# q of the odd heads by Strassen products ahead of the recurrence, and weight sums of the gates issued late

## The chip, the cores and the metric

The kernel runs on one core of a Trainium2 chip. The metric is the device time of one execution in microseconds; of several executions the median counts. The core has engines that work side by side, each through its own instructions in a fixed order: TensorE (PE: matmuls; its weight loads are shown apart as PEld), VectorE (DVE), ScalarE (ACT), GpSimd (POOL) and SyncE (SP). POOL and SP here mostly issue DMAs. An engine waits for another by semaphores.

## The reference

Two layers over 512 tokens with 16 meta tokens ahead of them (528 columns in the kernel), 2048 channels. The even layer joins a convolution module and a sparse attention of 8 heads, each multiplied by a gate, and projects the result out. The odd layer is a gated linear recurrence of 16 heads with a state of 128 by 128 each:

```python
def even_mixer(hn, w_in, ...):
    ...
    a_out = jax.nn.silu(layer_norm(u, ln_g, ln_b)) * jax.nn.silu(gate_a)
    ...
    b_out = b_out * jax.nn.silu(gate_b)
    return jnp.concatenate([a_out, b_out], axis=-1) @ w_out

def odd_mixer(hn, w_in, lb, norm_g, w_out):
    q, fz, i, g = split_last(hn @ w_in, (D_REC, D_REC, D_REC, D_REC))
    ...
    o = hgrn2_chunkwise(heads(jax.nn.silu(q)), heads(log_f), heads(k), heads(i))
    o = o * lax.rsqrt(jnp.mean(jnp.square(o), -1, keepdims=True) + RMS_EPS)
    ...
    return (o * silu(g)) @ w_out
```

All is float32. The change concerns q, one of the four projections of the odd layer: `hn @ w_in`, 2048 by 2048 for 512 tokens, 128 rows for each head.

## The kernel before

**Products in three matmuls.** To keep float32 precision each operand is split into a high half that TensorE takes as it is and a low half, the rest. `products` (L182 to L191) issues for each of eight slices of 128 channels three matmuls: high weights by high data (L188), high by low (L189), low by high (L190), 24 in all for one half stripe of weights (128 x 1024). `load_half` (L150 to L161) loads such a half on SP (L154), makes its high part on ACT (`wh`, L159) and its low part on DVE (`wl`, L160). `stripe` (L163) takes two halves for 128 rows of a projection.

**Strassen.** A pair of stripes against the two halves of the tokens (264 or 256 columns) can be had by seven products with half the columns, of sums of weights with sums of data ("forms": B11, B21, B22, N1, N2, T3, T4), where the plain way needs eight. The weight sums of products 7, 5, 6 and 3 are made in DRAM by `sum_step` (L246): a copying DMA (L258) and accumulating DMAs (L260) on POOL's queue. `some_steps` (L288) issues the next few of a list behind a given instruction. Lists: `steps` for the even layer's output, `gsteps` for q of the even heads and the output gates of heads 0 to 7 (`QPAIRS`, `GPAIRS`), `osteps` for the odd layer's output.

**Course of the program.** (1) The even layer's projections, scores, selection and the attention's heads; `gsteps` are issued behind steps of the scores, of the attention and of its last head (L551, L671, L735). (2) The eight gates of the convolution module (L774 to L787): `gate` (L604) runs a stripe, evacuates it with the norm's factor on DVE (L196), takes a tanh on ACT (L611) and multiplies on DVE (L612); then `z`, the module's output, is finished (L781 to L785). (3) The even layer's output projection: the pools of the attention are closed and a pool `xf` takes their place. `early_form0` makes the forms of the attention (tiles `sq`, loaded from DRAM by `attended` on POOL, L808, three buffers) and of `z`: high half `fh` on ACT (L205), low half `fl` on DVE (L206). The forms N2, N1, T3, T4 follow (L825 to L828, `xh` and `xl`). POOL also loads the residual (L844). Then 56 products in the order m = 2, 3, 1, 6, 5, 7, 4, each m for eight pairs (L864); what comes out is added to the residual on DVE, and `finish1` splits the new layer's input. (4) Head 0's projections, then Strassen products for q of the eight even heads and for eight gates (`strassen`, L982), from forms `gforms`; q of heads 12 and 14 goes to DRAM (`qd`), since there is no place for it. (5) The recurrence: for each of 16 heads `projections` (L950) runs the stripes fz, q (odd heads only) and v, and `rec_head` the recurrence itself; `head_inputs` (L1028) gives the tiles and loads q of heads 12 and 14 on SP. (6) Gates 8 to 15, forms, the odd layer's output by Strassen, the final norm.

**What sets the order.** A scheduler places instructions on each engine by a simulated timeline, with priority bands: weights (WGT) ahead of evacuation (EVAC), that ahead of SIDE (forms, pacing, heads' inner work) and CONV. Within an engine the order that comes out is fixed. Pools hold rings of buffers: a tile takes the place of an older one and waits for that one's last reader.

Of the kernel before, what the change touches and what calls it, by code (L numbers as in the profile page):

```python
# [72 lines left out]
def trunk_kernel(ctx: ExitStack, tc: tile.TileContext, x: bass.AP, w: bass.AP, wukv: bass.AP,  # L73
# [5 lines left out]
    def band(level):  # L79
        return tc.high_priority(level * 1000000)  # L80
# [171 lines left out]
    def sum_step(what, m, pair):  # L252

        a = {11: w[pair[0], 0], 12: w[pair[0], 1], 21: w[pair[1], 0], 22: w[pair[1], 1]}
        if what == "copy":
            dst = wsum[pair, m] = dram.tile([128, 1024], F32, name=f"ws{pair[0]}_{m}")
            src = {7: a[11], 5: a[21], 6: wsum.get((pair, 5)), 3: wsum.get((pair, 6))}[m]
            return (Q if m in (5, 7) and pair in EPAIRS else G).dma_start(dst, src)  # L258
        src = {7: a[21], 5: a[22], 6: a[11], 3: a[12]}[m]
        return G.dma_start(wsum[pair, m], src, accum_op=OP.add, max_dma_last_dim=4096)  # L260

    def product_weights(pair, m):
# [8 lines left out]
             for what, m in (("add", 7), ("add", 5), ("copy", 6), ("add", 6), ("copy", 3), ("add", 3))  # L271
             for pr in EPAIRS[g:g + 4]]
    QHEADS = tuple(range(0, 16, 2))
    QPAIRS = [tuple(S_FQV + 3 * h + 1 for h in QHEADS[i:i + 2]) for i in range(0, 8, 2)]
    GPAIRS = [(S_G + 2 * i, S_G + 2 * i + 1) for i in range(4)]
    gsteps = [(what, m, pr)
              for what, m in (("copy", 7), ("copy", 5), ("add", 7), ("add", 5),
                              ("copy", 6), ("add", 6), ("copy", 3), ("add", 3))
              for pr in QPAIRS]
    gsteps += [(what, m, pr)  # L280
               for what, m in (("copy", 7), ("copy", 5), ("add", 7), ("add", 5),
                               ("copy", 6), ("add", 6), ("copy", 3), ("add", 3))
               for pr in GPAIRS]
    osteps = [(what, m, pr) for pr in OPAIRS
              for what, m in (("copy", 7), ("copy", 5), ("add", 7), ("add", 5),
                              ("copy", 6), ("add", 6), ("copy", 3), ("add", 3))]
# [1 line left out]
    def some_steps(todo, n, behind):  # L288
        with tc.issue_after(behind.ins):
            for _ in range(min(n, len(todo))):  # L290
                sum_step(*todo.pop(0))

    def strassen_weights(pair, m, pool, at):

# [5 lines left out]
    bdram = dram.tile([HB, 16, BL], F32, name="bdram")  # L300
    mbd = dram.tile([HB, 128, T], F32, name="mbd")
    h1d = dram.tile([KT, 128, T], F32, name="h1d")
    qd = dram.tile([2, 128, SEQ], F32, name="qd")


    r1p = ctx.enter_context(tc.tile_pool(name="r1", bufs=KT, side="left", reuse_waits="tile"))
# [297 lines left out]
    def gate(s, dst, X, rstd, wide=True):  # L604

        ps = stripe(s, X, wide=wide)
        n = T if wide else SEQ
        a = et([128, T], F32, "gt", 3)
        with band(EVAC):
            evac(a[:, :n], ps, rstd)  # L610
            S.activation(dst, a[:, :n], AF.Tanh, scale=0.5)  # L611
            V.scalar_tensor_tensor(dst, dst, 1.0, a[:, :n], op0=OP.add, op1=OP.mult)  # L612
# [104 lines left out]
    def head(h):  # L717
        if h == 0:
            meta_tiles()
        if h % 2 == 0:  # L720
            with band(SIDE):
                kv.append(keys_values(h // 2))
        gb = et([128, T], F32, "gb", 2)
        gate(S_GQ + 2 * h, gb, X0, rstd0)
        ps = stripe(S_GQ + 2 * h + 1, X0)
        qh = et([128, T], F32, "qh", 2)
        with band(EVAC):
            evac(qh, ps, rstd0)
        Kh, Vt = [t[h % 2] for t in kv[-1]]
        with band(SIDE):  # L730
            for name, src in (("q", qh), ("k", Kh), ("g", gb)):
                S.activation(meta_of(name, h), src[:, :NM], AF.Copy)
            moved = G.dma_start(meta["v"][h * NM:(h + 1) * NM, :], Vt[:NM, 0, :])
            if h == HB - 1:
                some_steps(gsteps, 7, moved)  # L735
            if h == HB - 1:
                attend_meta()
            attend(h, qh, gb, Kh, Vt)
# [36 lines left out]
    for i in range(8):  # L775
        ga = et([128, T], F32, "gb", 2)
        gate(S_GA + i, ga, X0, rstd0)
        with band(SIDE):
            z = Z[i]
            V.tensor_tensor(z, z, rz, op=OP.mult)  # L780
            S.activation(z, z, AF.Identity, scale=col(V_LG + i), bias=col(V_LB + i))  # L781
            th = et([128, T], F32, "gt", 3)
            S.activation(th, z, AF.Tanh, scale=0.5)
            V.scalar_tensor_tensor(z, th, 1.0, z, op0=OP.add, op1=OP.mult)
            V.tensor_tensor(z, z, ga, op=OP.mult)  # L785
        MA.append(z)
# [79 lines left out]
    for at, (pr, m) in enumerate(turns):  # L866
        u, c0, c1 = us[pr], C[pr], C[8 + pr]
        o = (mps if at % 7 < 3 else ps1)()[:, :HT]
        with band(WGT):
            hi, lo = strassen_weights(EPAIRS[pr], m, xfp, at)  # L870
        products(o, hi, lo, forms0[FORM[m]], True, True)
        with band(EVAC):
            if m == 2:
                V.tensor_tensor(c0[:, LT], c0[:, LT], o, op=OP.add)
            elif m == 3:
                V.tensor_tensor(c0[:, RT], c0[:, RT], o, op=OP.add)
            elif m == 1:
                S.activation(u, o, AF.Copy)
                V.tensor_tensor(c0[:, LT], c0[:, LT], o, op=OP.add)
            elif m == 6:  # L880
                V.tensor_tensor(u, u, o, op=OP.add)
                V.tensor_tensor(c0[:, RT], c0[:, RT], u, op=OP.add)
            elif m == 5:
                V.tensor_tensor(c0[:, RT], c0[:, RT], o, op=OP.add)
                V.tensor_tensor(c1[:, RT], c1[:, RT], o, op=OP.subtract)
                finish1(pr)
            elif m == 7:
                V.tensor_tensor(u, u, o, op=OP.add)
                both = c1.rearrange("p (c t) -> p c t", c=2)
# [74 lines left out]
    def q_made(h):  # L964

        with band(EVAC):
            scaled(QT[h])
            if h >= 12:
                Q.dma_start(qd[h // 2 - 6], QT[h])

    def silu_gate(h):

# [6 lines left out]

    made = [0]  # L980

    def strassen(pairs, results, finished):  # L982

        act = None
        for m, pr in ((m, pr) for ms in ((1, 2, 3), (5,), (6,), (7,), (4,)) for pr in range(len(pairs)) for m in ms):
            o = (mps if made[0] % 7 < 3 else ps1)()[:, :HS]
            with band(WGT):
                hi, lo = strassen_weights(pairs[pr], m, gpp, made[0])
            made[0] += 1
            products(o, hi, lo, gforms[FORM[m]], True, True)  # L990
            (a, b), (aj, bj) = [[t[:, c * HS:(c + 1) * HS] for c in range(2)] for t in results[2 * pr:2 * pr + 2]]
            u = aj
            with band(EVAC):
                if m == 1:
                    S.activation(u, o, AF.Copy)
                elif m == 2:
                    V.tensor_tensor(a, u, o, op=OP.add)
                elif m == 3:
                    S.activation(b, o, AF.Copy)
                elif m == 5:  # L1000
                    V.tensor_tensor(b, b, o, op=OP.add)
                    S.activation(bj, o, AF.Copy, scale=-1.0)
                elif m == 6:
                    V.tensor_tensor(u, u, o, op=OP.add)
                    V.tensor_tensor(b, b, u, op=OP.add)
                    finished(2 * pr)
                elif m == 7:
                    V.tensor_tensor(u, u, o, op=OP.add)
                    V.tensor_tensor(bj, bj, u, op=OP.subtract)
                else:  # L1010
                    V.scalar_tensor_tensor(aj, u, -1.0, o, op0=OP.mult, op1=OP.subtract)
                    act = finished(2 * pr + 1)
        return act

    strassen(QPAIRS, [QT[h] for h in QHEADS], lambda n: q_made(QHEADS[n]))
    ON = [on_tile(h) for h in range(8)]
    act = strassen(GPAIRS, ON, silu_gate)
    with band(SIDE), tc.issue_after(act.ins):
        S.preload_act_table_set("natural_log_exp_and_others")
    gp.__exit__(None, None, None)  # L1020
# [6 lines left out]

    def head_inputs(h):  # L1028
        fz, v = [ht([128, T], F32, name, 2) for name in ("fz", "v")]
        if h in QT and h < 12:  # L1030
            return fz, QT[h], v
        q = ht([128, SEQ], F32, "q", 2)
        if h in QT:
            with band(WGT), tc.issue_after(loaded[0].ins):
                Q.dma_start(q, qd[h // 2 - 6])
        return fz, q, v

    hs = tc.tile_pool(name="hs", bufs=1, side="left", reuse_waits="tile")
# [505 lines left out]
```

## Time and profile before

| | |
|---|---|
| runs | 1882.87, 1882.13, 1880.12 us; median 1882.13 us |
| profiled execution | 1882.83 us, its span 1881.0 us |
| granted TensorE clock, mean | 0.998 |
| TensorE matmuls | 15347, busy 1864.0 us |
| DRAM traffic | 322.28 MB read, 112.41 MB written, 231 GB/s over the span |

A line of the page or of a view of the trace names an instruction by its line, engine, operation and the tiles that it writes and reads (`fl<-sq,fh`: fl from sq and fh), with its shape. A timeline row begins with the start and the duration in us; in brackets stands how long the engine sat idle before it and what it waited for. A row of the windows view begins with a stretch of the span and gives its length, the busy time of each engine with the number of its instructions, the granted clock, the mean share of the 16 DMA engines and GB/s. "L" numbers are lines of the kernel before; in the changed kernel the same code stands some lines further down (L205 and L206 stay, L612 is L622, L808 is L822, L844 is L858).

### The profile page before, as it was taken

The page shows a single profiled execution, that of the slowest core. Times are in us where ns is not written, and L with a number is a line of the kernel's source. Part 1 is how long each engine was busy: PE and PEld are TensorE (multiplying, and loading weights), DVE is VectorE, ACT ScalarE, POOL GpSimd, SP SyncE. Part 2 cuts the span into 40 slices and gives each one's busy share as a digit, 9 for nine tenths or more (in the row PEclk, how much of TensorE's full clock was granted, in tenths as well). Part 3 has the DMA queues.
Part 4 walks back from the last instruction along what each step waited for, and adds up shares of the span by engine and source line. Part 5 has one row for each costly group of instructions (what it writes and reads, how often), then busy time and mean ns, then how long its engine had stood idle before and what let it go on. Part 6 is the DMA issues. An engine that isn't in the chain of part 4 may idle for free.

```text
span 1881.0 us, 37954 instructions
## 1 busy us (share of the span) xinstructions
PE 1864.0 (99%) x15347; PEld 1792.7 (95%) x15347; DVE 1470.2 (78%) x2832; ACT 920.7 (49%) x1637; POOL 228.0 (12%) x379
## 2 busy tenths in 40 slices
PE   9999999999999999999999999999999999999997
PEld 8998899999999999999999999999999999889997
DVE  7599889997648569588875898878878787588777
ACT  6333532234433645456544655555555555346553
POOL 1020132123430212000000111000000100000000
PEclk9999999999999999999999999999999999999999
DMA  6578788889993857567655655534544544235665
GB/s 233 157 243 256 202 238 199 225 223 230 254 242 116 199 165 251 186 225 243 213 198 183 184 162 151 134 113 137 145 124 130 152 127 121 79 112 163 210 222 180
DMA packets 97776, 344.45 MB, mean 183 GB/s; under 512 B 14208, under 2 KB 22056, under 8 KB 96064
## 3 DMA queue, kind: packets, MB, share of 16 engines
q1 hardware_dynamic: 68272, 222.20, 35.2%
q0 software_dynamic: 29040, 119.63, 26.8%
q8 instruction: 120, 1.97, 0.4%
q14 instruction: 56, 0.46, 0.1%
q10 hardware_dynamic: 288, 0.19, 0.0%
HBM read 322.28 MB, written 112.41 MB: 231 GB/s over the span
## 4 chain that ended last, share of the span: by engine, by line
PE 92%; DVE 4%; DMA 2%; ACT 1%; issue 0%; SPq 0%; DVEq 0%; ACTq 0%
PE mps L189 22%; PE mps L188 22%; PE mps L190 22%; PE s L189 2%; PE s L188 2%; PE s L190 2%; PE sv L189 1%; DMA w<-in_w_dram 1%; PE sv L188 1%; PE sv L190 1%; PE po L703 1%; PE st L189 1%; PE st L188 1%; PE st L190 1%; PE s L1086 1%; DMA L<-mask 1%
## 5 line engine op out<-in xcount | busy, mean ns | idle before, releaser
L189 PE MATMUL mps<-xl,wh 128*128 128x264 f32 (+2 forms) x2928 | 883.2, 302 | 0.0
L188 PE MATMUL mps<-xh,wh 128*128 128x264 f32 (+2 forms) x2928 | 878.5, 300 | 2.5 <-DVE gt L196 2.1
L190 PE MATMUL mps<-xh,wl 128*128 128x264 f32 (+2 forms) x2928 | 880.8, 301 | 0.0
L159 ACT ACTIVATE wh<-w 128x1024 fp32r<-128x1024 f32 x361 | 382.7, 1060 | 545.1 <-PE mps L189 340.9
L188 PEld LDWEIGHTS mps<-xh,wh 128*128 128x128 f32 x2928 | 551.0, 188 | 20.5 <-DVE gt L196 2.7
L189 PEld LDWEIGHTS mps<-xl,wh 128*128 128x128 f32 x2928 | 551.6, 188 | 17.4 <-issue 0.6
L190 PEld LDWEIGHTS mps<-xh,wl 128*128 128x128 f32 x2928 | 551.1, 188 | 17.3
L160 DVE TENSOR_TENSOR wl<-w,wh 128x1024 fp32r<-128x1024 f32 x361 | 441.6, 1223 | 156.6 <-ACT wh L159 153.3
L600 DVE SCALAR_TENSOR_TENSOR z<-u,vec,z 128x528 f32<-128x528 f32 x240 | 181.1, 765 | 2.5
L260 POOL DMA_DIRECT2D ws<-in_w_dram x96 | 87.2, 1154 | 103.8 <-DMA ws<-ws 70.2
L189 PE MATMUL s<-xl,wh 128*128 128x256 f32 (+1 forms) x248 | 70.3, 283 | 0.0
L188 PE MATMUL s<-xh,wh 128*128 128x256 f32 (+1 forms) x248 | 70.2, 283 | 0.0
L190 PE MATMUL s<-xh,wl 128*128 128x256 f32 (+1 forms) x248 | 69.7, 281 | 0.0
L1169 DVE COPY_PREDICATED A<-msk,s 128x256 f32<-128x256 uint8 x96 | 47.0, 490 | 17.7 <-PE s L1088 16.9
L196 DVE TENSOR_TENSOR gt<-mps,rstd 128x264 f32<-128x264 f32 (+1 forms) x72 | 32.9, 458 | 30.4 <-PE mps L190 30.0
L663 POOL DMA_DIRECT2D L<-mask x32 | 30.3, 947 | 166.7 <-DMA L<-bdram 85.1
L1082 ACT ACTIVATE kt1h<-k 128x256 f16<-128x256 f32 x64 | 26.5, 414 | 42.7 <-DVE k L1175 41.9
L190 PEld LDWEIGHTS s<-xh,wl 128*128 128x128 f32 x248 | 46.8, 189 | 0.0
L189 PEld LDWEIGHTS s<-xl,wh 128*128 128x128 f32 x248 | 46.7, 188 | 0.1
L188 PEld LDWEIGHTS s<-xh,wh 128*128 128x128 f32 x248 | 46.7, 188 | 0.0
L1082 ACT ACTIVATE kt0h<-k 128x512 f16<-128x512 f32 (+1 forms) x64 | 33.0, 516 | 22.4 <-DVE k L1175 21.5
L565 DVE SCALAR_TENSOR_TENSOR mask<-sq,wiT,mask 128x264 f32<-128x264 f32 (+3 forms) x80 | 37.7, 494 | 7.1 <-ACT sq L564 6.2
(720 smaller groups left out, 3727.6 us busy)
## 6 DMA issues: line engine op xcount, KB each, us to landing
w<-in_w_dram SPq DMA_DIRECT2D x267, 512.0 KB, 3.9
ws<-in_w_dram POOLq DMA_DIRECT2D x128, 512.0 KB, 8.6
w<-ws SPq DMA_DIRECT2D x96, 512.0 KB, 3.5
ws<-ws POOLq DMA_DIRECT2D x48, 512.0 KB, 5.4
ws<-in_w_dram SPq DMA_DIRECT2D x16, 512.0 KB, 7.1
on<-h1d SPq DMA_DIRECT2D x30, 256.0 KB, 4.2
sq<-mbd POOLq DMA_DIRECT2D x16, 264.0 KB, 3.6
z<-in_x_dram SPq DMA_DIRECT2D x8, 264.0 KB, 4.9
```

Of the source, the lines that this page charges most:

```text
L159: S.activation(uh, used, AF.Copy)
L160: V.tensor_tensor(ul, used, uh.bitcast(F32), op=OP.subtract)
L188: P.matmul(o, hi[:, ws], xh, start=start and k == 0, stop=False)
L189: P.matmul(o, hi[:, ws], xl, start=False, stop=False)
L190: issued.append(P.matmul(o, lo[:, ws], xh, start=False, stop=stop and k == len(X) - 1))
L196: V.tensor_tensor(dst[:, sl.start - o:sl.stop - o], p[:dst.shape[0]], rstd[:dst.shape[0], sl], op=OP.mult)
L260: return G.dma_start(wsum[pair, m], src, accum_op=OP.add, max_dma_last_dim=4096)
L565: V.scalar_tensor_tensor(M[t][:, s0:s1], r[:, :s1 - s0], wiT[:, t, h:h + 1], M[t][:, s0:s1], op0=OP.mult, op1=OP.add)
L600: V.scalar_tensor_tensor(z, u[:, j:j + T], col(V_CW + i * CW + j), z, op0=OP.mult, op1=OP.add)
L663: return G.dma_start(biased[h, t][:, :wk(t)], M[t], accum_op=OP.add)
L1082: S.activation(hi, src, AF.Copy, scale=scale)
L1169: V.copy_predicated(A.rearrange("p b (n a m) -> p b n a m", a=2, m=mm)[:, :, :, 1, :], msk[:, li - 1 + i:li + i, :].rearrange("p b (n m) - ...
```

## The change

q of the odd heads, 8 stripes of 512 columns inside the recurrence, is now computed as four more pairs of Strassen products (`CPAIRS`) between those of the even heads' q and those of the gates. All eight results go to DRAM (`qd` has ten places), and `head_inputs` loads them on POOL. The weight sums of `CPAIRS` take the place that those of the gates had in `gsteps`. The gates' sums are a list of their own, `lsteps`, of 32 steps, issued by `paced_steps`: an ACT copy of one column of a tile that has just been made into a tile `pace`, a memset of that tile on POOL, and the DMAs behind that memset. They are issued three each at the attention's heads 6 and 7, one each at the gates 2 to 7 of the convolution module, one at each second pair of m = 1 in the even layer's output, and one behind every third product of q. The order of the gates' products is a little different too.

```diff
+    QDRAM = (12, 14) + tuple(range(1, 16, 2))
-    gsteps = [(what, m, pr)
+    gsteps = [(what, m, pr) for group in (QPAIRS, CPAIRS)
               for what, m in (("copy", 7), ("copy", 5), ("add", 7), ("add", 5),
                               ("copy", 6), ("add", 6), ("copy", 3), ("add", 3))
-              for pr in QPAIRS]
-    gsteps += [...
-               for pr in GPAIRS]
+              for pr in group]
+    lsteps = [(what, m, pr)
+              for what, m in (("copy", 5), ("copy", 7), ("add", 5), ("add", 7),
+                              ("copy", 6), ("add", 6), ("copy", 3), ("add", 3))
+              for pr in GPAIRS]
...
+    def paced_steps(todo, n, src, pool):
+
+        if not todo:
+            return
+        with band(SIDE):
+            p = pool.tile([128, 1], F32, name="pace", bufs=1)
+            S.activation(p, src[:, :1], AF.Copy)
+            some_steps(todo, n, G.memset(p, 0.0))
...
         gate(S_GQ + 2 * h, gb, X0, rstd0)
+        if h >= HB - 2:
+            paced_steps(lsteps, 3, gb, epools["es"])
...
         gate(S_GA + i, ga, X0, rstd0)
+        if i >= 2:
+            paced_steps(lsteps, 1, ga, epools["es"])
...
                 S.activation(u, o, AF.Copy)
+                if pr % 2:
+                    paced_steps(lsteps, 1, o, epools["ec"])
...
+            if made[0] % 3 == 2:
+                paced_steps(lsteps, 1, o, gpp)
...
+    strassen([(m, pr) for pr in range(4) for m in (1, 5, 2, 6, 3, 7, 4)], CPAIRS, odd, lambda n: q_made(2 * n + 1))
     ON = [on_tile(h) for h in range(8)]
-    act = strassen(GPAIRS, ON, silu_gate)
+    act = strassen(by_pass(((1, 2), (5,), (6,), (3,), (7,), (4,))), GPAIRS, lambda pr: ON[2 * pr:2 * pr + 2], silu_gate)
...
-        if h in QT and h < 12:
+        if h in QT and h not in QDRAM:
             return fz, QT[h], v
         q = ht([128, SEQ], F32, "q", 2)
         if h in QT:
-            with band(WGT), tc.issue_after(loaded[0].ins):
-                Q.dma_start(q, qd[h // 2 - 6])
+            G.dma_start(q, qd[QDRAM.index(h)])
```

The change also moves instructions that it doesn't name. ACT, around the convolution module's gates 4 and 5 (`gb<-gt` is the tanh of a gate, `fh<-sq` the high halves of the attention's forms, `fh<-z` those of the convolution's, `wh<-w` weights). Before:

```order
L783 ACTIVATE gt<-z 128x528
L205 ACTIVATE fh<-sq 128x264 x6
L159 ACTIVATE wh<-w_8037 128x1024
L611 ACTIVATE gb<-gt 128x528
L205 ACTIVATE fh<-sq 128x264 x6
L159 ACTIVATE wh<-w_8091 128x1024
L205 ACTIVATE fh<-sq 128x264 x2
L783 ACTIVATE gt<-z 128x528
L205 ACTIVATE fh<-sq 128x264 x2
L205 ACTIVATE fh<-z 128x264 x5
L159 ACTIVATE wh<-w_8159 128x1024
L611 ACTIVATE gb<-gt 128x528
```

ACT after, at the last two of those gates (L300 is the pace copy, L621 the tanh):

```order
L621 ACTIVATE gb<-gt 128x528
L300 ACTIVATE pace<-gb 128x1
L159 ACTIVATE wh<-w_8657 128x1024
L797 ACTIVATE gt<-z 128x528
L621 ACTIVATE gb<-gt 128x528
L300 ACTIVATE pace<-gb 128x1
L205 ACTIVATE fh<-sq 128x264 x6
L159 ACTIVATE wh<-w_8689 128x1024
L205 ACTIVATE fh<-sq 128x264 x10
L205 ACTIVATE fh<-z 128x264 x8
L159 ACTIVATE wh<-w_8721 128x1024
```

In the first piece the two tanh are those of gates 4 and 5, in the second those of gates 6 and 7. The 16 high halves of the attention's forms moved from around gate 4's tanh to behind the pace copy of the last gate.

DVE after, from the last gate's product on (L622 and L799; `fl<-sq` are the low halves, L888 the additions of the first three products, L839 a later form). In before the last of the 16 `fl<-sq` stood behind gate 5's evacuation, two gates earlier:

```order
L622 SCALAR_TENSOR_TENSOR gb<-gb,gt 128x528
L799 TENSOR_TENSOR z<-z,gb 128x528
L206 SCALAR_TENSOR_TENSOR fl<-sq,fh 128x264 x6
L160 TENSOR_TENSOR wl<-w_8689,wh 128x1024
L206 SCALAR_TENSOR_TENSOR fl<-sq,fh 128x264 x10
L839 SCALAR_TENSOR_TENSOR sq<-sq,z 128x264
L206 SCALAR_TENSOR_TENSOR fl<-z,fh 128x264 x2
L888 TENSOR_TENSOR qh<-qh,mps 128x264
L840 TENSOR_TENSOR z<-z 128x264
L888 TENSOR_TENSOR qh<-qh,mps 128x264
```

From there to the low half of the fifteenth product's weights (`wl_9076`) stand 87 operations of half a tile, 13 weight halves and one operation of a whole tile; the fourth product's low half (`wl_8724`) stands behind the whole tile and 33 of the rest.

TensorE after, at the first products (mps_8624 and mps_8656 are the outputs of the first two; from the fourth slice on the third, mps_8688, joins in), with numbers:

```order
L190 MATMUL mps_8198<-xh_250,wl_8256 128x264
L188 MATMUL mps_8624<-fh_8333,wh_8627 128x264
L188 MATMUL mps_8656<-fh_8333,wh_8659 128x264
L189 MATMUL mps_8624<-fl_8334,wh_8627 128x264
L190 MATMUL mps_8624<-fh_8333,wl_8628 128x264
L189 MATMUL mps_8656<-fl_8334,wh_8659 128x264
L190 MATMUL mps_8656<-fh_8333,wl_8660 128x264
L188 MATMUL mps_8624<-fh_8343,wh_8627 128x264
```

The first row is the last gate's last matmul, as in before. There one product followed the other: the first output's 24 matmuls, then those of the second.

More of the change, by code (lines that the diff above doesn't have):

```diff
@@ L273, in trunk_kernel @@
     QHEADS = tuple(range(0, 16, 2))
-    QPAIRS = [tuple(S_FQV + 3 * h + 1 for h in QHEADS[i:i + 2]) for i in range(0, 8, 2)]
+    QPAIRS, CPAIRS = [[tuple(S_FQV + 3 * h + 1 for h in (i + c, i + c + 2)) for i in range(0, 16, 4)] for c in range(2)]
+    QDRAM = (12, 14) + tuple(range(1, 16, 2))
     GPAIRS = [(S_G + 2 * i, S_G + 2 * i + 1) for i in range(4)]
-    gsteps = [(what, m, pr)
+    gsteps = [(what, m, pr) for group in (QPAIRS, CPAIRS)
               for what, m in (("copy", 7), ("copy", 5), ("add", 7), ("add", 5),
                               ("copy", 6), ("add", 6), ("copy", 3), ("add", 3))
-              for pr in QPAIRS]
-    gsteps += [(what, m, pr)
-               for what, m in (("copy", 7), ("copy", 5), ("add", 7), ("add", 5),
-                               ("copy", 6), ("add", 6), ("copy", 3), ("add", 3))
-               for pr in GPAIRS]
+              for pr in group]
[3 more added lines that the diff above has]
+              for pr in GPAIRS]
     osteps = [(what, m, pr) for pr in OPAIRS
@@ L302, in trunk_kernel @@
     h1d = dram.tile([KT, 128, T], F32, name="h1d")
-    qd = dram.tile([2, 128, SEQ], F32, name="qd")
+    qd = dram.tile([len(QDRAM), 128, SEQ], F32, name="qd")
     r1p = ctx.enter_context(tc.tile_pool(name="r1", bufs=KT, side="left", reuse_waits="tile"))
@@ L967, in q_made @@
             scaled(QT[h])
-            if h >= 12:
-                Q.dma_start(qd[h // 2 - 6], QT[h])
+            if h in QDRAM:
+                Q.dma_start(qd[QDRAM.index(h)], QT[h])
     def silu_gate(h):
@@ L980, in trunk_kernel, with strassen @@
     made = [0]
-    def strassen(pairs, results, finished):
+    def strassen(turns, pairs, results, finished):
         act = None
-        for m, pr in ((m, pr) for ms in ((1, 2, 3), (5,), (6,), (7,), (4,)) for pr in range(len(pairs)) for m in ms):
+        begun = set()
+        for m, pr in turns:
             o = (mps if made[0] % 7 < 3 else ps1)()[:, :HS]
@@ L990, in strassen @@
             products(o, hi, lo, gforms[FORM[m]], True, True)
-            (a, b), (aj, bj) = [[t[:, c * HS:(c + 1) * HS] for c in range(2)] for t in results[2 * pr:2 * pr + 2]]
+            if made[0] % 3 == 2:
+                paced_steps(lsteps, 1, o, gpp)
+            (a, b), (aj, bj) = [[t[:, c * HS:(c + 1) * HS] for c in range(2)] for t in results(pr)]
             u = aj
+            done = {m2 for m2, p2 in begun if p2 == pr}
+            begun.add((m, pr))
             with band(EVAC):
@@ L997, in strassen @@
                     V.tensor_tensor(a, u, o, op=OP.add)
[L998 to L1002, printed above, removed]
+                elif m in (3, 5):
+                    if done & {3, 5}:
+                        V.tensor_tensor(b, b, o, op=OP.add)
+                    else:
+                        S.activation(b, o, AF.Copy)
+                    if m == 5:
+                        S.activation(bj, o, AF.Copy, scale=-1.0)
                 elif m == 6:
@@ L1005, in strassen @@
                     V.tensor_tensor(b, b, u, op=OP.add)
-                    finished(2 * pr)
                 elif m == 7:
@@ L1011, in strassen, with by_pass, odd @@
                     V.scalar_tensor_tensor(aj, u, -1.0, o, op0=OP.mult, op1=OP.subtract)
+                if m != 4 and done | {m} >= {2, 3, 5, 6} and not done >= {2, 3, 5, 6}:
+                    finished(2 * pr)
+                elif m == 4:
                     act = finished(2 * pr + 1)
         return act
-    strassen(QPAIRS, [QT[h] for h in QHEADS], lambda n: q_made(QHEADS[n]))
+    def by_pass(passes):
+        return [(m, pr) for ms in passes for pr in range(4) for m in ms]
+    strassen(by_pass(((1, 2, 3), (5,), (6,), (7,), (4,))), QPAIRS, lambda pr: [QT[h] for h in QHEADS[2 * pr:2 * pr + 2]],
+             lambda n: q_made(QHEADS[n]))
+    def odd(pr):
+        for h in (4 * pr + 1, 4 * pr + 3):
+            if h not in QT:
+                QT[h] = on_tile(h % 8 // 2)
+        return QT[4 * pr + 1], QT[4 * pr + 3]
+    strassen([(m, pr) for pr in range(4) for m in (1, 5, 2, 6, 3, 7, 4)], CPAIRS, odd, lambda n: q_made(2 * n + 1))
     ON = [on_tile(h) for h in range(8)]
-    act = strassen(GPAIRS, ON, silu_gate)
+    act = strassen(by_pass(((1, 2), (5,), (6,), (3,), (7,), (4,))), GPAIRS, lambda pr: ON[2 * pr:2 * pr + 2], silu_gate)
     with band(SIDE), tc.issue_after(act.ins):
```

## The prediction

> **What bounds the kernel now.** I read the page's head first, the shares of the span and of the chain that ended last.
>
> ```profile
> span 1881.0 us, 37954 instructions
> PE 1864.0 (99%) x15347; PEld 1792.7 (95%) x15347; DVE 1470.2 (78%) x2832; ACT 920.7 (49%) x1637; POOL 228.0 (12%) x379
> PE 92%; DVE 4%; DMA 2%; ACT 1%; issue 0%; SPq 0%; DVEq 0%; ACTq 0%
> ```
>
> TensorE has hardly a gap, and the chain runs over it. So a matmul that goes saves its spacing to the next, and a microsecond in which TensorE waits is lost. The "mean ns of one" of a group overlaps with its neighbours; the spacing comes from windows full of one width (columns: TensorE busy and its matmuls, weight loads, DVE, ACT, POOL, granted clock, DMA share, GB/s). The first lies in the odd layer's Strassen products, 256 columns wide, the second in the output gates at the end of the recurrence, 512 wide.
>
> ```profile
> 920.00:1040.00 120.00, 120.00 (x1024) 120.00 (x1023) 79.92 (x107) 55.17 (x73) 0.00 (x0) 1.00 0.58 189
> 1650.00:1690.00 40.00, 40.00 (x175) 32.45 (x174) 34.94 (x71) 17.50 (x31) 0.00 (x0) 1.00 0.38 126
> ```
>
> That is 120.00/1024 = 0.117 us for 256 columns and 40.00/175 = 0.229 us for 512.
>
> **The change, part by part. One: fewer columns for q.** It removes 8 stripes x 2 halves x 24 = 384 matmuls of 512 columns, 384 x 0.229 = 87.8 us, and adds 4 pairs x 7 products x 24 = 672 of 256 columns, 672 x 0.117 = 78.8 us. The difference is 9.0; a window's edges cut a matmul on each side, so 0.229 can be up to 0.232 (40.00/172.5), and the difference 10.4. I take **-10**, with bounds -9 and -10.8. The weight halves grow from 16 to 28; their splitting lies on ACT and DVE, which have room in the added stretch (DVE 79.92 of 120.00 in the first window, which holds such products with their splits).
>
> The Trainium skill speaks against this step: "TensorE: Matmul & The Clock Gate", section "Back-to-back issue gap", gives about 81 ns for sustained matmuls of 128 columns and about 131 ns for 512, so a wide one would be far cheaper by the column. By it the removed ones are worth 50 us and the added ones, at an interpolated 98 ns (an estimate from that page), 66 us: this part would cost 15 us. The two windows above disagree, at 229 against 117 ns, and the measurement decides; I give that case no chance.
>
> **Two: the start of the even layer's output projection.** TensorE passes from the last gate to the first product without a pause (timeline of TensorE):
>
> ```profile
> 716.26 0.28 PE L190 MATMUL mps<-xh,wl 128*128 128x264 f32 x1
> 716.38 0.28 PE L188 MATMUL mps<-fh,wh 128*128 128x264 f32 x1
> ```
>
> It can, since the halves of the 16 forms of the attention (fh on ACT, fl on DVE) are made long before, while gates 4 and 5 run. First and last row of DVE's timeline that make them:
>
> ```profile
> 679.57 0.77 DVE L206 SCALAR_TENSOR_TENSOR fl<-sq,fh 128x264 fp32r<-128x264 f32 x2
> ...
> 692.15 0.77 DVE L206 SCALAR_TENSOR_TENSOR fl<-sq,fh 128x264 fp32r<-128x264 f32 x2
> ```
>
> In the changed order all of them stand behind the pace copy of gate 7 on ACT, and behind that gate's last DVE operations. Both engines work in order, so no form can be ready before gate 7 is evacuated. The chain from its last matmul takes its durations from these rows of DVE and ACT around it:
>
> ```profile
> 716.58 0.43 DVE L196 TENSOR_TENSOR gt<-mps,rstd 128x264 f32<-128x264 f32 x1
> ...
> 717.61 1.22 DVE L160 TENSOR_TENSOR wl<-w,wh 128x1024 fp32r<-128x1024 f32 x1
> 718.75 0.43 DVE L827 SCALAR_TENSOR_TENSOR z<-sq,z 128x264 f32<-128x264 f32 x1
> 719.09 0.43 DVE L206 SCALAR_TENSOR_TENSOR xl<-sq,xh 128x264 fp32r<-128x264 f32 x1
> 719.44 0.43 DVE L827 SCALAR_TENSOR_TENSOR z<-sq,z 128x264 f32<-128x264 f32 x1
> 719.78 0.70 DVE L612 SCALAR_TENSOR_TENSOR gb<-gb,gt 128x528 f32<-128x528 f32 x1
> 717.74 0.63 ACT L611 ACTIVATE gb<-gt 128x528 f32<-128x528 f32 x1
> 720.40 1.04 ACT L205 ACTIVATE xh<-z 128x264 fp32r<-128x264 f32 x3
> ```
>
> Evacuation to 717.01, tanh 0.63, product 0.70: 718.4. The pace copy of one column isn't in this trace; between nothing and the 0.41 of a copy of 264 columns I take 0.2. From 718.6 ACT makes an fh every 0.315 us ((1.04 - 0.41)/2, from the last row), DVE an fl every 0.345 (718.75 to 719.09 to 719.44). Only three of the eight attention tiles are loaded by then: the ring `sq` has three buffers, and POOL loads the next when both fl of an older one are done. That wait, and the time from issue to landing (tile view of `sq`), in before:
>
> ```profile
> 680.63 0.54 POOL L808 DMA_DIRECT2D sq<-mbd  x1 [13.50 <-DVE fl L206]
> DMA to landing us min/median/max: 3.0/3.6/4.8
> ```
>
> So tiles 3 to 5 are issued at 720 to 722 and land near 725.5, are split by 726.5, and tiles 6 and 7 land near 730.5 and are split by 732. The first three products, which the new order interleaves, end there instead of at 716.38 + 72 x 0.12 = 725.0: **7 us** late. POOL's loads of the residual stand ahead of these, but are issued early; they cost nothing here.
>
> Then DVE is late. Between gate 7's last product and the low half of the fifteenth product's weights the new order holds on DVE 87 operations of half a tile (0.345 us each, 30.0), 13 weight halves (717.61 to 718.75: 1.14 each, 14.8) and one of a whole tile (0.6): 45.4 us, and the two landings add about 6 us in which it has nothing to do. From 719.1 that is 770.5. In before the fifteenth product begins 14 x 24 x 0.12 = 40.3 us after 716.38, at 756.7. So TensorE starts it **14 us** late, the 7 among them. The windows of before on either side show that DVE had no room for such a debt:
>
> ```profile
> 680.00:720.00 40.00, 40.00 (x331) 40.00 (x330) 35.36 (x77) 21.93 (x46) 9.10 (x17) 1.00 0.64 207
> 720.00:760.00 40.00, 40.00 (x331) 40.00 (x330) 34.37 (x64) 20.47 (x33) 4.84 (x9) 1.00 0.78 250
> ```
>
> It works 35.36 and 34.37 of 40 us; in the change 24 fl (8.3 us) leave the first window, where it will idle, and enter the second. Bounds: +6 if only the first wait counts, +18 if every later landing takes 4.8 and is waited for. Nearest to these rows is **+14**. The third product's own weights also wait for the pace of gate 7 (their buffer lies over its tile); at 719 plus a landing of some 4 us that is before the forms, so it adds nothing.
>
> **Three: the recurrence.** With q gone from the odd heads, TensorE gets shorter there and DVE becomes the busier one. Windows of a pair of heads, early to late, and DVE's groups in the later ones:
>
> ```profile
> 1095.00:1168.00 73.00, 73.00 (x737) 69.75 (x736) 66.35 (x159) 42.62 (x80) 7.10 (x12) 1.00 0.52 145
> 1168.00:1240.81 72.81, 72.81 (x699) 69.78 (x698) 60.48 (x137) 40.66 (x76) 5.76 (x11) 1.00 0.48 131
> 1240.81:1313.45 72.64, 72.64 (x697) 69.67 (x697) 58.45 (x132) 38.99 (x72) 5.77 (x10) 1.00 0.48 131
> 1458.42:1531.00 72.58, 72.58 (x696) 69.61 (x696) 57.80 (x131) 38.80 (x72) 5.77 (x10) 1.00 0.48 132
> L160 DVE TENSOR_TENSOR wl<-w,wh 128x1024 fp32r<-128x1024 f32 x40 | 48.9, 1223 | 6.8 <-ACT wh L159 6.6
> L196 DVE TENSOR_TENSOR q<-mps,rstd 128x512 f32<-128x512 f32 x4 | 2.8, 690 | 2.4 <-PE mps L190 2.4
> ```
>
> Each pair loses 48 x 0.229 = 11.0 us on TensorE and 2 x 1.22 + 0.69 = 3.1 on DVE. Late pairs then hold 61.6 on TensorE and 55.3 on DVE (90%), the pair from 1168 on 61.8 and 57.4 (93%), the first one 62.0 and 63.2. TensorE stays full beside a DVE as busy as 37.89 of 40 (95%):
>
> ```profile
> 1120.00:1160.00 40.00, 40.00 (x387) 37.33 (x384) 37.89 (x91) 23.92 (x44) 4.55 (x7) 1.00 0.51 135
> ```
>
> So only the first pair loses, 63.2 - 62.0 = **+1.2**, with bounds 0 (its surplus is worked off later) and 63.2/0.95 - 62.0 = +4.5. The loads of q stand well ahead of their heads on POOL, which is busy 5.77 of 72.64 there.
>
> **Four: transfers and pacing.** One Strassen product lasts 24 x 0.117 = 2.8 us and loads 0.5 MB; a weight sum behind every third product adds 0.5 MB per 8.4 us, some 62 GB/s on the 189 of the window above. TensorE stands through more than that:
>
> ```profile
> 840.00:880.00 40.00, 40.00 (x333) 40.00 (x332) 32.75 (x46) 20.61 (x26) 3.79 (x7) 1.00 0.74 245
> 480.00:520.00 40.00, 40.00 (x328) 39.37 (x327) 23.12 (x42) 18.73 (x46) 16.34 (x25) 1.00 1.02 260
> ```
>
> The last sum is issued about 26 products (73 us) ahead of its use. The 32 pace copies, 0.2 us each on an ACT at half load, and as many memsets on POOL lie beside products; without that cover 32 x 0.2 = 6 us. I take **0**, bounds 0 and +2.
>
> The sum is -10 + 14 + 1.2 + 0 = +5.2 us on the profiled execution's 1882.83 (its span of 1881.0 and 1.8 around it); that execution lies 0.7 above the median of 1882.13, so the forecast is **1887.3**, and 1887 rounded.
>
> **The rivals.** Each differs from the sum in one term.
> - A, the debt is not there: only the first wait counts, as DVE catches up while TensorE drains products with weights in hand: -10 + 6.5 + 1.2 = -2.3, 1879.8. For it: ACT and DVE idle while TensorE does gates 4 to 7, and some work may slip forward. Against: both engines work in order.
> - B, no wait at all: parts one and three alone leave -10 + 0 = -10, 1872.1 on the median. It needs forms ahead of gate 7, which the order contradicts, or landings and splits hidden by work that I don't see.
> - C, slower still: DVE bounds the recurrence. Decides if its waits between operations (6.8 and 2.4 us ahead of two groups above) stay when TensorE shortens: above about 95% of its time. Price: 63.2/0.95 - 62.0 - 1.2 = 3.3 in the first pair and up to 1 in each of three others, 6 in all: 1893.
> - D, the clock: the granted clock falls after TensorE has stopped, and not in a short pause.
>
> ```profile
> 1868.00:1870.00 2.00, 1.48 (x8) 0.88 (x7) 1.52 (x5) 0.83 (x2) 0.00 (x0) 1.00 0.77 257
> 1872.00:1874.00 2.00, 0.00 (x0) 0.00 (x0) 2.00 (x7) 0.00 (x0) 0.00 (x0) 0.50 0.71 245
> 340.00:344.00 4.00, 2.42 (x20) 2.21 (x20) 3.96 (x12) 0.00 (x0) 1.58 (x3) 1.00 0.42 137
> ```
>
> The waits for two landings in part two are longer than the 1.6 us of the last row. At 0.50 the matmuls behind them, 9 to 27 of 0.12 us, take twice as long: up to 3 us, half of it hidden as TensorE waits for DVE anyway: +1.5, 1888.8. The Trainium skill, "TensorE: Matmul & The Clock Gate", section "What's actually happening", puts the fall to half rate after an idle window of about 3.4 us; the rows above agree roughly: the clock is at 0.50 from 2 us after a window in which TensorE still worked.
>
> That the odd heads' q is not really moved can be ruled out by the order.
>
> **How the numbers follow.** Chances: forecast 0.48, A 0.25, B 0.12, C 0.10, D 0.05. The forecast's own bounds, 10 to 18 for part two and 0 to 4.5 for part three, give 1882 to 1892. A measurement of this kernel can tell about 0.2% (3.8 us) from no change. Slower by more means above 1885.9: three quarters of the forecast (0.36), C and D (0.15), 0.51. Within: the rest of the forecast (0.12) and most of A (0.20), 0.32. Faster: B and the rest of A, 0.17. The range 1876 to 1894 takes in A, C, D and the bounds of the unknown costs, and leaves out B and 0.05 above.
>
> **What would show it.** In the profile of the changed kernel: a TensorE window of 716 to 772 with some 42 us busy (14 lost), no fl of an attention tile before 718, DVE above 90% from 732 to 770; in the recurrence pairs of heads 61 to 62 us apart, with DVE near 90%; full windows in the added Strassen stretch, of 78 to 79 us. Wrong would be: fl rows ahead of gate 7's evacuation, a first wait followed by full TensorE windows (A), pairs that stay above 63 us (C), or a granted clock below 1.00 near 730 (D).

## The result, and the profile after

| | runs | median us |
|---|---|---|
| kernel before | 1880.12 to 1882.87 (4) | 1881.49 |
| changed kernel | 1889.92 to 1897.88 (4) | 1893.31 |
| ratio | 95% interval 1.0041 to 1.0088 | 1.0064 |

The change costs 11.8 us, where +5.2 was forecast; the interval of the ratio lies clear of 1. The profiled execution took 1889.92 us, the least of the four runs, so it shows the places of the loss better than their full size. The page's first rows look hardly different (columns as before):

```profile
span 1888.2 us, 38782 instructions
PE 1863.7 (99%) x15635; PEld 1808.2 (96%) x15635; DVE 1482.8 (79%) x2872; ACT 935.4 (50%) x1689; POOL 257.8 (14%) x449
```

TensorE is as busy as before with 288 more matmuls, since narrower ones took the place of wide ones and some ran at a lower clock; what is lost is in one place. Two windows of 40 us from the end of the last gate on, first of the kernel before, then of the changed one:

```profile
716.38:756.38 40.00, 40.00 (x332) 40.00 (x331) 35.66 (x70) 22.20 (x36) 5.40 (x11) 1.00 0.81 263
```

```profile
713.81:753.81 40.00, 30.33 (x191) 28.32 (x190) 31.35 (x71) 21.83 (x49) 9.56 (x18) 0.83 0.69 226
```

332 matmuls became 191, and the granted clock 0.83. The missing 141 are 141 x 40.00/332 = 17.0 us. TensorE's timeline there shows the waits in turn, each with what ended it:

```profile
713.69 0.28 PE L190 MATMUL mps<-xh,wl 128*128 128x264 f32 x1
716.59 0.51 PE L188 MATMUL mps<-fh,wh 128*128 128x264 f32 x2 [2.62 <-ACT fh L205]
...
722.08 0.39 PE L188 MATMUL mps<-fh,wh 128*128 128x264 f32 x1 [2.81 <-ACT wh L159]
...
723.34 0.59 PE L190 MATMUL mps<-fh,wl 128*128 128x264 f32 x1 [0.74 <-DVE wl L160]
...
732.51 0.29 PE L190 MATMUL mps<-fh,wl 128*128 128x264 f32 x1
734.20 0.39 PE L188 MATMUL st<-fh,wh 128*128 128x264 f32 x1 [1.40 <-ACT wh L159]
...
738.08 0.59 PE L190 MATMUL st<-fh,wl 128*128 128x264 f32 x1 [1.21 <-DVE wl L160]
...
740.22 0.42 PE L190 MATMUL st<-fh,wl 128*128 128x264 f32 x1
740.44 0.42 PE L188 MATMUL st<-fh,wh 128*128 128x264 f32 x1
```

The first form comes 2.9 us after the last gate matmul. The first three products end at 732.6, 10.1 us later than 72 spacings of 0.12 after 713.81. The fourth product's low weights come at 738.08, and from there matmuls run 0.22 us apart (740.22 to 740.44) where full windows have 0.12. ACT shows why the forms come late (its timeline):

```profile
715.95 0.20 ACT L300 ACTIVATE pace<-gb 128x1 f32<-128x1 f32 x1 [0.84 <-DVE gb L622]
716.12 1.99 ACT L205 ACTIVATE fh<-sq 128x264 fp32r<-128x264 f32 x6
720.97 1.06 ACT L159 ACTIVATE wh<-w 128x1024 fp32r<-128x1024 f32 x1 [2.86 <-DMA w<-in_w_dram]
724.77 2.06 ACT L205 ACTIVATE fh<-sq 128x264 fp32r<-128x264 f32 x6 [2.75 <-DMA sq<-mbd]
729.31 1.38 ACT L205 ACTIVATE fh<-sq 128x264 fp32r<-128x264 f32 x4 [2.47 <-DMA sq<-mbd]
```

All 16 `fh` stand behind the pace copy of gate 7, in three rounds of the ring of three buffers, and two rounds wait for their DMA.

### The profile page after: what moved, and what is told of

Read it like the earlier page. It is cut to its first block, busy times and chain, and to the rows that moved or that the text cites. A ratio compares the mean times of both kernels' runs of the same rounds, so it can differ in the third digit from the quotient of the medians.

```text
span 1888.2 us, 38782 instructions
## 1 busy us (share of the span) xinstructions
PE 1863.7 (99%) x15635; PEld 1808.2 (96%) x15635; DVE 1482.8 (79%) x2872; ACT 935.4 (50%) x1689; POOL 257.8 (14%) x449
## 4 chain that ended last, share of the span: by engine, by line
PE 91%; issue 4%; DVE 2%; DMA 1%; ACT 1%; POOL 0%; SPq 0%; DVEq 0%; POOLq 0%; ACTq 0%
PE mps L188 22%; PE mps L190 21%; PE mps L189 21%; PE s L189 2%; PE s L188 2%; PE s L190 2%; PE po L713 1%; PE sv L189 1%; PE sv L188 1%; PE sv L190 1%; PE st L190 1%; PE st L189 1%; PE st L188 1%; PE s L1122 1%; PE po L1245 1%
## 5 line engine op out<-in xcount | busy, mean ns | idle before, releaser
L189 PE MATMUL mps<-xl,wh 128*128 128x264 f32 (+2 forms) x2856 | 847.5, 297 | 0.0
L190 PE MATMUL mps<-xh,wl 128*128 128x264 f32 (+2 forms) x2856 | 846.6, 297 | 0.2 <-DVE wl L160 0.2
L188 PE MATMUL mps<-xh,wh 128*128 128x264 f32 (+2 forms) x2856 | 845.6, 296 | 1.0 <-DVE gt L196 0.5
L159 ACT ACTIVATE wh<-w 128x1024 fp32r<-128x1024 f32 x373 | 395.0, 1060 | 543.9 <-PE mps L189 293.9
L160 DVE TENSOR_TENSOR wl<-w,wh 128x1024 fp32r<-128x1024 f32 x373 | 455.6, 1222 | 203.3 <-ACT wh L159 200.3
L188 PEld LDWEIGHTS mps<-xh,wh 128*128 128x128 f32 x2856 | 537.8, 188 | 13.6 <-DVE gt L196 1.1
L189 PEld LDWEIGHTS mps<-xl,wh 128*128 128x128 f32 x2856 | 538.0, 188 | 12.3 <-issue 0.6
L190 PEld LDWEIGHTS mps<-xh,wl 128*128 128x128 f32 x2856 | 537.6, 188 | 12.6 <-DVE wl L160 0.4
L260 POOL DMA_DIRECT2D ws<-in_w_dram x112 | 102.6, 1147 | 113.7 <-DMA ws<-ws 72.2
L258 POOL DMA_DIRECT2D ws<-ws x56 | 35.4, 656 | 63.7 <-DMA ws<-in_w_dram 53.8
```

The costliest lines, as they stand in the source:

```text
L159: S.activation(uh, used, AF.Copy)
L160: V.tensor_tensor(ul, used, uh.bitcast(F32), op=OP.subtract)
L188: P.matmul(o, hi[:, ws], xh, start=start and k == 0, stop=False)
L189: P.matmul(o, hi[:, ws], xl, start=False, stop=False)
L190: issued.append(P.matmul(o, lo[:, ws], xh, start=False, stop=stop and k == len(X) - 1))
```

## The experiments

Two theories stood against each other: that the place of the pace tile (pool `es`, closed ahead of the forms' pool `xf`) sets the order and the order costs the time, or that the weight sums issued at the gates crowd out the loads. All medians are from runs beside the kernel before (1881.49 to 1881.98 in these sets). The four combinations and what they measured:

| | sums at gates 2 to 7 | no sums there |
|---|---|---|
| a pace in `es` at the gates | 1893.31, again 1892.72 | 1889.11 |
| none in `es` there | 1878.78 | 1874.93 |

**Tile in another pool.** Edit (`em` stays open through the even layer's output):

```diff
-            paced_steps(lsteps, 1, ga, epools["es"])
+            paced_steps(lsteps, 1, ga, epools["em"])
```

> The changed kernel with one word changed: at the convolution module's gates the tile of the pace copy lies in the pool em, which stays open through the even layer's output, instead of es, which is closed ahead of it. Copies, memsets and sums stay. Theory (the tile in es holds all forms back behind gate 7): the stall of 17.2 us that the changed kernel's trace shows between 713.8 and 745 us goes, the first form matmul follows the last gate matmul within 0.3 us, and the median falls by 15 to 20 us to about 1875, below the kernel before by 6 to 9. Rival 1 (the weight sums issued at the gates crowd out the forms' and weights' loads): the sums are the same, so 1890 to 1894 stays. Rival 2 (the copies on ScalarE and memsets on GpSimd themselves): also 1890 to 1894.

Measured: 1878.78 us (1876.6 to 1885.42, 12 runs), ratio 0.9985 (0.9977 to 0.9994). The time falls by 14 us with the sums in place, and the first form matmul follows the last gate's (717.76) at 717.88 without a wait: the order is the main cause. It did not reach 1875, and in its profiled execution (1882.36, 3.6 above the median) the window after the last gate was not full. That window, and ScalarE's waits for loads of weights from 715 to 745 (total in us, number, longest):

```profile
717.88:757.88 40.00, 35.54 (x282) 34.37 (x281) 34.60 (x71) 20.50 (x35) 7.41 (x15) 1.00 0.88 283
ACT wh L159 <- DMA w<-in_w_dram: 7.0, 2, 4.6
```

282 of 332 matmuls: 50 x 0.1205 = 6.0 us lost, at full clock. ScalarE waited 7.0 us for weights, 4.6 in one wait, while the DMA engines stood at a share of 0.88. That is a second cost, beside the order. (Without sums at the gates, below, the same row reads 2.0 in one wait, and TensorE waits for nothing there.)

**Pace alone on the kernel before.** Edit, with `es`, then with `em` in its place:

```diff
+    def pace_only(src, pool):
+        with band(SIDE):
+            p = pool.tile([128, 1], F32, name="pace", bufs=1)
+            S.activation(p, src[:, :1], AF.Copy)
+            G.memset(p, 0.0)
...
         gate(S_GA + i, ga, X0, rstd0)
+        if i >= 2:
+            pace_only(ga, epools["es"])
```

> The kernel before with only the pace copies and memsets at gates 2 to 7, in the pool es, with no weight sum behind them; all else as before. Theory: the stall alone, about 17 us with the slower clock in it: 1897 to 1901. Rival 1 (the sums' transfers): 1880 to 1884. Rival 2 (the copies and memsets themselves): also slower, so only the next run tells it from the theory.

> As the run before, with the tile in the pool em. Theory: 1880 to 1884, as before, since a copy of one column takes 0.2 us on a ScalarE at half load. Rival 2: as slow as with es.

Measured: 1897.08 with `es` (1896.16 to 1897.64, ratio 1.0078, 1.0063 to 1.0092) and 1882.83 with `em` (1880.96 to 1886.02, ratio 1.0007, 0.9998 to 1.0016). The same six copies of one column and six memsets cost 14.3 us more in one pool than in the other, where they cost nothing measurable, and no transfer was added. So neither the copies nor the sums make this part; the pool does. The window after the last gate, with `es`:

```profile
714.58:754.58 40.00, 30.62 (x190) 28.48 (x190) 30.42 (x69) 22.04 (x49) 8.68 (x17) 0.79 0.61 203
```

190 matmuls, as in the changed kernel (191), though q is as before.

**The changed kernel once more.**

> The changed kernel once more, to see a second trace and how far its runs lie apart: 1889 to 1898. If the granted clock at the stall differs from run to run, the spread comes from there; the runs without a stall should then lie within 3 us of each other.

Three runs lay between 1892.12 and 1892.78; a fourth took 3814.01 us, which no other run here resembles and for which I have no explanation. The wide spread of the first set did not come again, so that it comes from the clock isn't shown.

**No sums at the gates.** Edit: the pace at the gates goes, and heads 6 and 7 issue six sums each.

```diff
-            paced_steps(lsteps, 3, gb, epools["es"])
+            paced_steps(lsteps, 6, gb, epools["es"])
...
-        if i >= 2:
-            paced_steps(lsteps, 1, ga, epools["es"])
```

> The changed kernel with no pace and no sum at the convolution module's gates 2 to 7; their six sums go to the attention's heads 6 and 7, six each in place of three. The forms are then made beside gates 4 and 5 again. In the run with the tile in em a wait of 5.3 us was left between 723 and 741 us of its trace (ScalarE's wh waited up to 4.6 us for a weight load, with the DMA engines at a share of 0.94). Theory (the sums of the gates, 0.5 MB each, crowd the loads at the start of the output projection): that wait goes too, the median is 1872 to 1876, and the profile shows under 1 us lost between 715 and 760. Rival (the wait is of another cause, such as the odd heads' sums in the same list or the residual's loads): 1877 to 1880, as with em.

Measured: 1874.93 (1873.48 to 1875.43), ratio 0.9963 (0.9949 to 0.9976), 3.9 us below the run with sums and `em`. The window after the last gate is full again:

```profile
714.19:754.19 40.00, 40.00 (x332) 40.00 (x331) 35.75 (x70) 22.22 (x36) 5.37 (x11) 1.00 0.80 266
```

**Tile in es, sums elsewhere.** Edit: at the gates `paced_steps([None], 0, ga, epools["es"])`, six sums each at heads 6 and 7.

> The changed kernel with its pace copies and memsets at gates 2 to 7 in es, but without the six sums behind them, which go to heads 6 and 7 (six each). It is the fourth of four combinations: tile in es or not, sums at the gates or not; the other three measured 1893.0 (es, sums), 1878.8 (em, sums), 1874.9 (neither). If the two costs add up (14.2 for the order, 3.9 for the sums), 1889.1. If the sums' transfers lie hidden in the stall that the order makes, 1893. If the order's cost is mostly the sums landing among the loads that the stall waits for, below 1886.

Measured: 1889.11 (1888.08 to 1893.39), ratio 1.0042 (1.0028 to 1.0056). The table adds up: the tile's pool costs 14.2 without the sums and, by the mean of the two sets of the changed kernel (1893.0), 14.2 with them; the sums with their pacing cost 3.9 in either row by the medians. This 3.9 is less firm than the 14.2. With the tile in `es` the intervals of the ratios overlap (1.0028 to 1.0056 without the sums, 1.0040 to 1.0070 and 1.0041 to 1.0088 with them); with `em` or none they just part (0.9977 to 0.9994 and 0.9949 to 0.9976), and that pair holds the copies and memsets too, which alone measured +0.85, within the noise.

**The clock.** Two attempts to keep TensorE busy in its waits:

```diff
+    def keep_busy(n, behind):
+        p = pso()
+        with band(WGT + 1), tc.issue_after(behind.ins):
+            for _ in range(n):
+                P.matmul(p[:, :128], ones_d, ones_d, start=True, stop=True)
...
-        products(o, hi, lo, forms0[FORM[m]], True, True)
+        issued = products(o, hi, lo, forms0[FORM[m]], True, True)
+        if at == 1:
+            keep_busy(12, issued[2])
+        elif at == 2:
+            keep_busy(6, issued[7])
```

(26 and 14 matmuls in the first attempt.)

> The changed kernel with 40 matmuls of 128 x 128 that nothing uses put into the two waits of TensorE at the start of the output projection: 26 behind the ninth matmul of the second product, 14 behind the last of the third. Theory (the halved clock after these waits costs 2 to 3 us on the path, since 21 matmuls behind the fourth product's weights take 0.22 us each instead of 0.12): the granted clock between 720 and 750 us is above 0.95 (0.66 to 0.85 without them) and the median 2 to 3 us below the changed kernel's, about 1890. Rival (the halved clock hides behind VectorE and the loads): the clock rises and the time stays at 1892 to 1894.

> The changed kernel again with unused matmuls in TensorE's waits, fewer than before, since each of 128 x 128 took two passes of 0.115 us there: 12 (2.8 us) in the wait of 2.8 us ahead of the third product's weights, 6 (1.4 us) in the wait of 1.4 us ahead of the fourth's. Theory (the halved clock costs 2 to 3 us): the granted clock between 720 and 750 us stays above 0.9, and the median falls to 1890 or 1891. Rival (hidden): 1892 to 1894 with the higher clock.

Measured: 1893.59 (1891.63 to 1893.86) and 1894.65 (1893.26 to 1897.02): no gain. In the first attempt the added matmuls ran longer than the waits (26 of them became 52 entries in 5.97 us), so it tells nothing. In the second they fit, and the clock was higher at first; behind the next waits it fell as in the changed kernel. Its windows, then the changed kernel's for the same stretches (the last gate ends 1.0 us later in the attempt):

```profile
720.00:730.00 10.00, 8.38 (x66) 8.13 (x66) 3.38 (x7) 3.12 (x7) 2.41 (x5) 0.96 0.93 293
730.00:740.00 10.00, 6.54 (x42) 5.16 (x40) 8.23 (x22) 8.08 (x19) 1.08 (x2) 0.90 0.29 87
740.00:750.00 10.00, 10.00 (x64) 10.00 (x65) 10.00 (x21) 4.15 (x8) 1.60 (x3) 0.76 0.70 232
```

```profile
720.00:730.00 10.00, 7.17 (x33) 6.65 (x34) 3.61 (x8) 3.81 (x10) 1.62 (x3) 0.66 0.88 279
730.00:740.00 10.00, 6.51 (x38) 5.57 (x37) 9.96 (x24) 7.83 (x19) 1.08 (x2) 0.81 0.30 91
740.00:750.00 10.00, 10.00 (x73) 10.00 (x73) 10.00 (x24) 5.70 (x11) 3.22 (x6) 0.85 0.80 276
750.00:760.00 10.00, 10.00 (x85) 10.00 (x84) 10.00 (x21) 5.33 (x11) 1.07 (x2) 1.00 0.88 280
```

Between 720 and 730 a clock of 0.96 in place of 0.66 won nothing: there TensorE waits for forms anyway. Between 740 and 750 TensorE has no wait, and 73 matmuls stand where a window at full clock has 85: 12 x 0.12 = 1.4 us on the path, and 21 x 0.12 = 2.5 in the attempt. Fine slices show this second fall in both traces: to 0.50 from 736.2 to 743.0 in the changed kernel, from 737.9 to 744.8 in the attempt. It is as long in both, and more of it lies behind 740 in the attempt. What the clock costs in all was not isolated.

**Other places for the six sums.** One kernel issues three sums each at heads 6 and 7 and two behind every five products of q (`made[0] % 5 in (1, 3)`); another issues eight each at the heads and none in the even layer's output.

> As the run without sums at the gates, with the six sums moved back and not forward: three each at heads 6 and 7, and two behind every five products of q in place of one behind every third (last use unchanged). Theory: the same 1872 to 1876, as the products' stretch has room for it (a window of the kernel before was full at 245 GB/s). If the stretch of q's products loses time under the denser sums, 2 to 5 us more.

> As the run with no sums at the gates (1874.9), and none in the even layer's output either: eight each at heads 6 and 7, one behind every third product of q as in the change. That run's trace still loses 2.1 us between 795 and 880 us on weight loads. Theory (the sums there cause it): 1872 to 1874. Rival (residual writes and loads cause it): 1875, or more if eight sums at a head disturb the attention.

Measured: 1876.48 (1874.44 to 1879.38) and 1876.07 (1874.56 to 1877.62). Both medians lie just above 1874.93. The runs of the first spread over 5 us, and its profiled execution was the slowest of its ten (1879.38). There TensorE waited in the stretch of q's products, which the kernel without sums at the gates passes without a gap. First the denser sums, then none at the gates:

```profile
990.00:1030.00 40.00, 36.63 (x300) 35.41 (x299) 23.89 (x32) 16.04 (x25) 3.63 (x10) 1.00 0.84 264
990.00:1030.00 40.00, 40.00 (x342) 40.00 (x341) 24.95 (x32) 15.54 (x23) 3.05 (x8) 1.00 0.80 254
```

42 matmuls, 4.9 us, are missing, as the expectation had named for denser sums. The second kernel did remove the lost time that it aimed at, in the traces of the two (no sums at the gates first, then sums at heads):

```profile
780.00:890.00 110.00, 108.36 (x883) 107.55 (x882) 89.05 (x132) 60.57 (x78) 10.53 (x20) 1.00 0.71 237
```

```profile
780.00:890.00 110.00, 110.00 (x903) 109.71 (x902) 90.52 (x133) 62.50 (x81) 8.64 (x16) 1.00 0.66 227
```

20 matmuls, 2.4 us, were won there and did not show in the median. In these two traces the last gate's last matmul starts at 714.07 and at 715.80, so 1.7 us were lost ahead of it; whether the eight sums at the heads cause that isn't shown. The best kernel of the study remains the one without sums at the gates: 6.8 us faster than before and 18.1 below the changed kernel.

## Why the prediction was right, and where it was not

The sign, the place and the range hold, the range narrowly: the median lies 0.7 below its upper end, and two of the four runs lie above it. The sum is 6.6 us too small. By its own steps:

| step | forecast | measured | from |
|---|---|---|---|
| q and the recurrence | -10 + 1.2 = -8.8 | -6.8 | no sums at the gates against before |
| forms behind gate 7 | +14 | +14.2 | tile in es against em or none, three pairs |
| transfers and pacing | 0 | +3.9 | sums at the gates against none |
| sum | +5.2 | +11.3 | 11.8 and 10.7 in the two sets |

**Transfers were the term that failed.** I priced the sums in the Strassen stretch and found room. That holds: the changed kernel's window there is full at a higher rate than any row I had quoted from a Strassen stretch.

```profile
960.00:1080.00 120.00, 120.00 (x1023) 120.00 (x1023) 79.61 (x110) 49.16 (x69) 9.72 (x23) 1.00 0.85 259
```

But six sums are issued at the gates, the last of them right ahead of the stretch in which POOL and SP load forms, residual and weights at once. Here TensorE waits for a load that lands late, while in the full Strassen window it waits for none. My bound of +2 had been drawn from stretches of the other kind. Even there the room ends: two sums behind every five products in place of one behind every three lost 4.9 us in one trace, above.

**The forms behind gate 7: right in size, right in its first half, wrong in its second.** The chain of evacuation, tanh, product, pace copy (0.20 us) and `fh` came as worked out: first form matmul 2.9 us after the last gate's. (The first `fl` stands at 716.57, ahead of the 718 that I had named, as the last gate ended 2.6 us earlier than in before.) Three products ended 10.1 us late, not 7. One cause is that the second round of `sq` was waited for to 724.77, though POOL issued the first of its loads at 717.8:

```profile
716.72 0.91 POOL L260 DMA_DIRECT2D ws<-in_w_dram  x1
717.29 0.91 POOL L858 DMA_DIRECT2D gb<-in_x_dram  x1
717.83 1.97 POOL L822 DMA_DIRECT2D sq<-mbd  x3
DMA to landing us min/median/max: 2.9/3.4/7.1
```

The sum is issued just ahead of them, and the slowest landing of `sq` grew from 4.8 to 7.1 us. With the tile in `es` and the sums elsewhere it was 4.4, the second round began at 722.12, and the three products ended 8.3 us late. The debt of DVE that I spread to the fifteenth product was collected at once, at the fourth: its `wl` stands behind 33 operations, so TensorE waited until 738.08, and from 750 on windows are full (85 matmuls) beside a DVE at 10.00. The scheduler had put the later weights ahead of the later forms, so a busy DVE held nobody up. The clock then took part of what my second half had taken: rival D's mechanism did occur, and so did its sign, a granted clock below 1.00 near 730. That 14 stands beside a measured 14.2 is so in part luck: the first half was larger than worked out, the second came at another place, and the halved clock had no part in the term.

On the clock the Trainium skill, "TensorE: Matmul & The Clock Gate", section "What's actually happening", gives an idle window of about 3.4 us. Here it fell behind shorter waits, of 2.62 and 2.81 us with 2.7 us of work between them, and in the second trace of the same kernel in the first of them already (last section); so the measurement decides. The steps of 3.41 us in which it changes here agree with the page in length; that such a window must be idle does not show.

**q and the recurrence.** DVE did not become the bound. The busiest stretch of the recurrence, with no sums at the gates:

```profile
1210.00:1265.00 55.00, 55.00 (x609) 53.95 (x608) 52.83 (x131) 37.14 (x70) 6.33 (x11) 1.00 0.58 151
```

DVE works 96% of it and TensorE has no gap, so rival C falls, and no wait shows for my +1.2. What part one saved can be read from TensorE's rows: the first and the last Strassen matmul for q and gates, and the last matmul of the output gates behind the recurrence, first in the kernel before, then in the changed one:

```profile
937.63 0.28 PE L188 MATMUL st<-gh,wh 128*128 128x256 f32 x1
1062.05 0.28 PE L190 MATMUL s<-gh,wl 128*128 128x256 f32 x1
1707.53 0.39 PE L190 MATMUL mps<-xh,wl 128*128 128x512 f32 x1
```

```profile
952.87 0.28 PE L188 MATMUL st<-gh,wh 128*128 128x256 f32 x1
1156.32 0.28 PE L190 MATMUL s<-gh,wl 128*128 128x256 f32 x1
1715.26 0.39 PE L190 MATMUL mps<-xh,wl 128*128 128x512 f32 x1
```

The Strassen stretch grew from 124.42 to 203.45 us, by 79.0, as the 78.8 of part one has it. The stretch behind it fell from 645.48 to 558.94, by 86.5, and not by the 87.8 to 89 of the matmuls that went. So this step is worth -7.5 and not -8.8; without sums at the gates the two lengths are the same within 0.01 us. Part one's -10 was 2.5 too much; its plain 9.0 lay nearer. Why the second stretch gives 1.3 to 2.5 us less than its matmuls, with no wait of TensorE in it, stays open. The -6.8 of the table is a difference of medians and holds the stretches ahead too: in its trace the kernel without sums at the gates reaches the end of gate 7 2.2 us earlier than before and loses 2.5 us from there to the Strassen stretch (780 to 890, above).

Rival A (only the first wait) and B (no wait) are excluded by the 17 us of the window and by the pair on the kernel before.

## What to carry to other kernels

A tile of one column can cost 14 us through the pool that it is put in: if that pool is closed ahead of work that was made early, the tile's last user becomes the gate for all of it. After such an edit compare the order of instructions around every place where pools are closed. And price added transfers at the place where they are issued, not where there is room: sums of 0.5 MB behind every third product of q left TensorE without a wait, two behind every five lost 4.9 us in one trace, and six issued at the gates, ahead of a start that waits for its loads, cost 3.9 us by the medians, however these divide among the six.

## What was not expected of the hardware

The granted clock halved after a wait shorter than 3 us. The changed kernel's TensorE waits 2.62 us for the first form. Slices behind that wait and behind the next one, of 2.81 us, in its first trace:

```profile
717.00:718.00 1.00, 1.00 (x8) 0.94 (x8) 1.00 (x5) 1.00 (x4) 1.00 (x3) 1.00 0.63 97
722.00:723.00 1.00, 0.52 (x2) 0.30 (x2) 0.94 (x1) 0.03 (x1) 0.00 (x0) 0.75 1.00 319
723.00:724.00 1.00, 0.66 (x3) 0.67 (x4) 0.28 (x1) 0.00 (x0) 0.00 (x0) 0.50 1.03 418
```

In its second trace (the changed kernel once more) the wait of 2.62 us ends at 717.38:

```profile
716.00:717.00 1.00, 0.00 (x0) 0.00 (x0) 0.97 (x2) 0.26 (x2) 0.06 (x1) 0.87 0.33 131
717.00:718.00 1.00, 0.62 (x3) 0.62 (x3) 1.00 (x3) 1.00 (x4) 1.00 (x3) 0.50 0.04 8
```

There one wait of 2.62 us was enough; in the first trace the clock stood through it and fell behind the second. Slices of 0.1 us show where it changes: it falls at 722.5 and 736.2 and rises at 729.3 and 743.0 in the first trace, falls at 716.7 and 737.2 and rises at 730.4 and 744.1 in the second. Within a trace these times lie multiples of 3.41 us apart (the second attempt to keep TensorE busy has the shortest such step, from the fall at 717.46 to the rise at 720.88). So it is likely that the place of a wait against such steps decides, and that this place differed between the two executions. How little work in a step brings the clock down isn't settled: in the traces of this case falls stand behind steps in which TensorE was busy for 0.20 to 0.75 of the time, and one step with 0.49 has no fall.

The kernel before ran through a single wait of 1.58 us at full clock (window 340 to 344). And a float32 matmul of 128 x 128 on plain tiles shows as two entries of 0.115 us (26 as 52 in 5.97 us).
